# Mixture-of-experts stage: expert pairs in four 32-column strips with raw fp32 weights, in place of single experts with split weights

## The chip, the cores and the metric

The kernel runs on one core of one Trainium2 chip. The metric is device time in microseconds of one execution. Before the change three runs took 1139.29, 1140.35 and 1140.89 us (median 1140.35).

## What is computed

Two transformer blocks run one after the other on 256 tokens of width 1024. The change touches the last part of the second block alone, a hierarchical mixture of experts:

```python
def hier_moe(h, lp):
    g_logits = h @ lp['w_router_group'] + lp['b_router_group']       # 4 groups
    g_sel = argmax(g_logits); p_sel = softmax(g_logits)[g_sel]
    e_sel = (h @ lp['w_router_expert'] + lp['b_router_expert'])[group g_sel]   # 4 experts
    top_v, top_i = lax.top_k(e_sel, 2)
    w_top = softmax(top_v) * p_sel
    for e in range(16):
        a = silu(h @ w_gate[e]) * (h @ w_up[e])      # 1024 -> 512
        y = y + combine[..., e, None] * (a @ w_down[e])   # 512 -> 1024
```

Each token goes to one group of four experts and to two experts in it. Each expert has three fp32 matrices of 2 MB, so the stage reads 16 x 3 x 2 = 96 MB of weights.

## The kernel before

Up to the router the kernel runs the first block's two layers and the second block's mixer; this part has the same instructions in both kernels. The stage in question is the function `moe`.

**Precision.** A matrix product is made of three passes in the type fp32r: weights `raw` are loaded by a DMA of 1 MB, ScalarE casts them to `whi` (L191), VectorE forms the rest `wlo` (L192), and `mm3` (L247) multiplies hi by hi, hi by lo and lo by hi. The activations are split in the same way (`xgh`/`xgl`, `ahh`/`ahl`).

**Order of the work.** `route` (L1210 on) forms the logits `lt`, gives each token its group and a slot of 128 in that group (`slot`), and the weight of each expert (`comb`). `gather` (L1281) brings the tokens of two groups into slots by matmuls with a 0/1 matrix `oh`, 256 columns at a time. Then for each of 16 experts come `expert_gate`, `expert_split` (L1328 transposes), `expert_up` and `expert_out`, software-pipelined by one expert, each with 128 slots as the stationary side and 512 columns as the moving side: 72 matmuls an expert. After each group `combine` (L1354) adds the result to the tokens in `y`. `finish` (L1445 to L1457) normalizes, adds the residual and stores.

**Buffers.** All weight DMAs stand in one queue, that of SyncE (SP), in program order, each of 1 MB (`128x2048` fp32). `raw()` chooses the buffer: three in the pool `wraw`, and others in the pools `wx`, `s8` and `act3`. The split weights lie in `wsp` (three buffers of `whi` and `wlo`), which lives to the end of the kernel. `cst3`, a table of the mixer, occupies one `wraw` buffer until its last use at L982.

**Too many tokens.** When a group has over 128 tokens, a further pass runs under `If(rv > 0)` (L1421): every engine loads the flag (L1420) and branches.

Of the kernel before, what the change touches and what calls it, by code (L numbers as in the profile page):

```python
# [19 lines left out]
NEG = -1e30  # L20
SPREAD = (0, 2, 4, 6, 1, 3, 5, 7)
# [121 lines left out]
class Build:  # L143
    def __init__(self, ctx, tc, ins, out, offs, dbg=None):
        self.tc, self.nc, self.ins, self.out, self.dbg = tc, tc.nc, ins, out, dbg or {}
        self.offs, self.at = offs, {}
        pool = lambda name, bufs, **k: ctx.enter_context(tc.tile_pool(name=name, bufs=bufs, **k))
        self.const = pool("const", 1, side="right")
        self.wraw = pool("wraw", 3)
        self.psum = pool("psum", 1, space=bass.MemoryType.PSUM)  # L150
        self.pool = pool
        self.pending = None
        self.wx, self.wy, self.nraw = None, None, 0
# [40 lines left out]
    def raw(self, shape):  # L194
        n, self.nraw = self.nraw, self.nraw + 1
        if self.wx:
            i = n % 10 if n < 20 else (n - 20) % 6
            if i == 8:
                return self.big("raw", shape[1:])
            if i >= 6:  # L200
                return self.act.tile(shape, F32, tag=("xgh", "xgl", None, "yo")[i - 6], name="raw", bufs=1 if i == 9 else 2)
            if i >= 4:
                return self.wx.tile(shape, F32, tag="raw", name="raw")
        else:
            i = n % 4
        if self.wy and i == 3:
            return self.wy.tile(shape, F32, tag="raw", name="raw")
        return self.wraw.tile(shape, F32, tag="raw", name="raw")
# [1002 lines left out]
    def route(self):  # L1211
# [9 lines left out]
        rank = self.ranks(v[:, 0:2], 2, "g")  # L1221
        asg = tmp.tile([P, 2, 4], FR, tag="asg", name="asg", bufs=1)
        nc.vector.tensor_scalar(asg, rank, 0.0, None, op0=OP.is_equal)
        own = asg.bitcast(F32)
        ps = self.bank()
        nc.tensor.matmul(ps[:, 0:8], self.striu, asg.rearrange("p j g -> p (j g)"), start=True, stop=False,
                         skip_group_check=True)
        nc.tensor.matmul(ps[:, 4:8], self.onesr, asg[:, 0], start=False, stop=True, skip_group_check=True)
        self.slot = keep.tile([P, 2, 4, 4], F32, tag="slot", name="slot")[:, :, :, 0]
        nc.vector.tensor_scalar(self.slot, own, -1000.0, 1000.0, op0=OP.mult, op1=OP.add)  # L1230
        self.slotted = tt(self.slot, self.slot, ps[:, 0:8].rearrange("p (j g) -> p j g", j=2), op=OP.add)
        for j in range(2):
            nc.tensor.matmul(ps[:, 8:12], self.onesr, asg[:, j], start=j == 0, stop=j == 1, skip_group_check=True)
# [7 lines left out]
        rank = self.ranks(ve, 8, "e")  # L1241
# [19 lines left out]
        self.split(comb, *(self.idc[:, :, o:o + 16].rearrange("p j (g i) -> p j g i", g=4) for o in (P, P + 16)))  # L1261
        self.over = keep.tile([P, 5], mybir.dt.int32, tag="over", name="over")
        mxc = small("mxc", 1)
        nc.vector.tensor_reduce(mxc, ps[:, 8:12], AX.X, OP.max)
        nc.vector.tensor_scalar(self.over[:, 0:4], ps[:, 8:12], 128.0, None, op0=OP.is_gt)
        nc.vector.tensor_scalar(self.over[:, 4:5], mxc, 128.0, None, op0=OP.is_gt)

    def gather(self, p, slot):
        nc = self.nc
        oh = self.act.tile([P, 2, 2, P], FR, tag="oh", name="oh", bufs=2)  # L1270
        for j in range(2):
            nc.vector.tensor_tensor(oh[:, j], self.p("iota")[:, None, :].to_broadcast([P, 2, P]),
                                    slot[:, j, 2 * p:2 * p + 2, None].to_broadcast([P, 2, P]), op=OP.is_equal)
        X = self.hilo("xg", 8, 256, bufs=2)
        yield oh, X
        for q in range(4):
            ps = self.bank()
            for k in range(2):
                f = slice((2 * q + k) * P, (2 * q + k + 1) * P)
                for i, (j, s) in enumerate(((0, 0), (1, 0), (0, 1), (1, 1))):  # L1280
                    nc.tensor.matmul(ps[:, k * 256:(k + 1) * 256], self.H2[s][:, j, f],  # L1281
                                     oh[:, j].rearrange("p n s -> p (n s)"), start=i == 0, stop=i == 3)
            t = self.act.tile([P, 2, 256], F32, tag="xgt", name="xgt", bufs=2)
            for k in range(2):
                m = 2 * q + k
                nc.scalar.activation(t[:, k, :], ps[:, k * 256:(k + 1) * 256], AF.Identity, bias=self.cols[:, 2, m:m + 1],
                                     scale=self.cols[:, 1, m:m + 1])
            self.split(t, X[0][:, 2 * q:2 * q + 2], X[1][:, 2 * q:2 * q + 2])
            yield

    def select(self, g, oh):
        nc = self.nc
        ps = self.bank()
        for j in range(2):
            nc.tensor.matmul(ps[:, j * 160:(j + 1) * 160], oh[:, j, g % 2, :], self.idc[:, j, :], start=True, stop=True)
        v = ps[:, 0:320].rearrange("p (j s) -> p j s", j=2)
        oT = self.act.tile([P, 2, P], FR, tag="oT", name="oT", bufs=2)
        nc.scalar.copy(oT, v[:, :, 0:P])
        cw = self.act.tile([P, 4], F32, tag="cw", name="cw", bufs=2)
        for i in range(4):  # L1300
            e = 4 * g + i
            nc.vector.tensor_reduce(cw[:, i:i + 1], v[:, :, P + e:P + 32:16], AX.XY, OP.add)
        return oT, cw

    def expert_in(self, name, e, X):
        w = self.ins[name][e].rearrange("q p (k c) -> p q k c", k=4)
        n = slice(e // 4 % 2 * P, (e // 4 % 2 + 1) * P)
# [7 lines left out]
    def expert_gate(self, e, X):  # L1315
        ga = self.tmp.tile([P, 512], F32, tag="ga", name="ga")
        self.nc.scalar.activation(ga, self.expert_in("w_gate_2", e, X), AF.Silu)
        return ga

    def expert_up(self, e, X, ga, cw):  # L1320
        self.nc.vector.scalar_tensor_tensor(ga, self.expert_in("w_up_2", e, X), cw[:, e % 4:e % 4 + 1], ga,
                                            op0=OP.mult, op1=OP.mult)

    def expert_split(self, ga):
        nc = self.nc
        ps = self.bank()
        for m in range(4):
            nc.tensor.transpose(ps[:, m * P:(m + 1) * P], ga[:, m * P:(m + 1) * P], self.c("ident"))  # L1328
        A = self.hilo("ah", 4, P, bufs=2)
        self.split(ps.rearrange("p (m s) -> p m s", m=4), *A)  # L1330
        return A

    def expert_out(self, e, A, acc):
        w = self.ins["w_down_2"][e].rearrange("q p (k c) -> p q k c", k=2)
        for q in range(2):
            W = self.weights(w[:, q], 2, 1024, -2 if e else -4)
            for hf in range(2):
                self.mm3(acc[hf], [((A[0][:, 2 * q + k, :], A[1][:, 2 * q + k, :]),
                                    (W[0][:, k, hf * 512:(hf + 1) * 512], W[1][:, k, hf * 512:(hf + 1) * 512]))
                                   for k in range(2)], start=e % 4 == 0 and q == 0, stop=e % 4 == 3 and q == 1)  # L1340

    def group_out(self, acc):
# [18 lines left out]
    def moe(self, x2, h2):  # L1361
        nc = self.nc
        self.H2 = h2
        self.held = []
        self.idc = self.act.tile([P, 2, 160], FR, tag="idc", name="idc")
        so = self.tmp.tile([P, 2, P], FR, tag="ga", name="so")
# [6 lines left out]
        it = self.gather(0, self.slot)  # L1373
        got = next(it)
        with self.tc.issue_after(self.slotted.ins):
            self.h2lo()
        for _ in it:
            pass
        self.held = [self.h2hi.ins]
        ga = self.expert_gate(0, got[1])  # L1380
        sel = self.select(0, got[0])
        self.expert_up(0, got[1], ga, sel[1])
        self.held = []
        done = None
        for e in range(16):
            g = e // 4
            if e < 15:
                if e == 7:
                    for _ in it:
                        pass  # L1390
                    got = nxt
                gn = self.expert_gate(e + 1, got[1])
            if e % 4 == 0:
                acc = [self.bank("acc", 4) for _ in range(2)]
            A = self.expert_split(ga)
            if done:
                with self.later(100):
                    self.combine(y, *done)
                done = None
            if e == 13:  # L1400
                g2 = [self.act.tile([P, 512], F32, tag=f"g2{q}", name="g2") for q in range(2)]
                self.row(self.cols[:, 3, :], g2)
            if e < 15:
                nsel = self.select(g + 1, got[0]) if e % 4 == 3 else sel
                self.expert_up(e + 1, got[1], gn, nsel[1])
                ga = gn
            if e == 3:
                it = self.gather(1, self.slot)
                nxt = next(it)
# [165 lines left out]
```

## Time and profile before

| | before |
|---|---|
| median of 3 runs | 1140.35 us |
| the profiled execution | 1136.58 us |
| its span, first to last instruction | 1134.7 us |
| mean granted TensorE clock | 0.975 of full |
| TensorE busy / VectorE / ScalarE | 95% / 79% / 57% |
| read from device memory | 246.01 MB |

The profiled execution is 1.88 us longer than its span, and 3.77 us shorter than the median of the runs. Times below are counted from the first instruction of the span.

### The profile page before, as it was taken

The numbers are of one execution on the slowest core, as the hardware profiler recorded it, in microseconds if no ns is written. First come the engines' busy times: TensorE is split into PE (matmuls) and PEld (weight loads), VectorE is DVE, ScalarE is ACT, GpSimd is POOL, SyncE is SP. The second block draws the span as 40 slices with busy tenths as digits, with TensorE's granted clock in tenths as the row PEclk, the third lists the DMA queues.
The fourth block names the chain that finished last, engine by engine and source line by source line (L and its number), as shares of the span: only waits on it lengthen the run. The fifth ranks groups of instructions, "written<-read, shape, count | busy, mean of one in ns | idle before, by whom it ended". The sixth has DMA issues, their size and how long they took to land.

```text
span 1134.7 us, 18470 instructions
## 1 busy us (share of the span) xinstructions
PE 1073.8 (95%) x7384; PEld 974.0 (86%) x7384; DVE 894.6 (79%) x1448; ACT 643.5 (57%) x937; POOL 130.2 (11%) x139
## 2 busy tenths in 40 slices
PE   7997999999999989899999989899899999999995
PEld 6896999999998978899999988877788888878783
DVE  6897678888777977856877778775599888998976
ACT  5635554344455364635554345743687778777763
POOL 3190010000020930310000022000000000000001
PEclk9998999999999989989999999899899999999998
DMA  8634347776754244555667750320678689989871
GB/s 283 232 112 167 131 152 275 247 254 242 268 187 149 103 158 154 213 189 210 236 237 283 294 207 24 144 75 12 265 274 339 259 323 344 350 345 371 302 299 41
DMA packets 41390, 248.34 MB, mean 219 GB/s; under 512 B 4560, under 2 KB 6992, under 8 KB 15312
## 3 DMA queue, kind: packets, MB, share of 16 engines
q1 hardware_dynamic: 41296, 247.08, 59.0%
q8 instruction: 60, 0.98, 0.3%
q14 instruction: 34, 0.28, 0.1%
HBM read 246.01 MB, written 1.05 MB: 218 GB/s over the span
## 4 chain that ended last, share of the span: by engine, by line
PE 46%; DVE 4%; ACT 2%; issue 1%; POOL 1%; POOLq 0%; DVEq 0%; ACTq 0%
PE mm L247 23%; PE acc L247 14%; DVE wlo L192 1%; ACT whi L191 1%; PE mm L1354 1%; PE mm L1281 1%; PE mm L733 1%; PE mm L1328 1%; PE acc L922 1%; PE mm L805 0%; POOL ssq L285 0%; PE mm L1063 0%; PE mm L1064 0%; DVE Mt L757 0%; PE mm L1129 0%
## 5 line engine op out<-in xcount | busy, mean ns | idle before, releaser
L191 ACT CAST whi<-raw 128x1024 fp32r<-128x1024 f32 (+2 forms) x375 | 406.0, 1124 | 262.2 <-PE mm L247 124.7
L192 DVE TENSOR_TENSOR wlo<-raw,whi 128x1024 fp32r<-128x1024 f32 (+2 forms) x375 | 484.2, 1326 | 80.5 <-ACT whi L191 79.4
L247 PE MATMUL mm<-hfh,whi 128*128 128x256 f32 x672 | 91.5, 278 | 0.1
L247 PE MATMUL mm<-hfl,whi 128*128 128x256 f32 x672 | 90.4, 277 | 0.0
L247 PE MATMUL mm<-hfh,wlo 128*128 128x256 f32 x672 | 90.1, 277 | 0.0
L285 POOL TENSOR_TENSOR ssq<-ssq,sqt 128x256 f32<-128x256 f32 x40 | 38.2, 957 | 430.1 <-ACT sqt L277 428.8
L247 PEld LDWEIGHTS mm<-hfh,whi 128*128 128x128 f32 x672 | 83.2, 188 | 0.4 <-ACT whi L191 0.4
L247 PEld LDWEIGHTS mm<-hfl,whi 128*128 128x128 f32 x672 | 82.7, 188 | 0.0
L247 PEld LDWEIGHTS mm<-hfh,wlo 128*128 128x128 f32 x672 | 82.7, 188 | 0.0
L247 PE MATMUL acc<-ffh,whi 128*128 128x256 f32 x352 | 72.0, 285 | 0.0
L247 PE MATMUL mm<-whi,xgh 128*128 128x512 f32 x256 | 71.7, 399 | 0.4 <-ACT xgh L191 0.3
L247 PE MATMUL acc<-ffh,wlo 128*128 128x256 f32 x352 | 71.0, 283 | 0.0
L247 PE MATMUL acc<-ffl,whi 128*128 128x256 f32 x352 | 70.7, 282 | 0.0
L247 PE MATMUL mm<-wlo,xgh 128*128 128x512 f32 x256 | 70.4, 395 | 0.0
L247 PE MATMUL mm<-whi,xgl 128*128 128x512 f32 x256 | 70.0, 395 | 0.0
L696 DVE CUSTOM_DVE_ANT_0 araw<-araw,arow 128x1024 f32<-128x1024 f32 x48 | 58.5, 1231 | 0.0
L247 PEld LDWEIGHTS mm<-wlo,xgh 128*128 128x128 f32 x256 | 47.9, 187 | 11.9 <-DVE wlo L192 0.3
L247 PEld LDWEIGHTS mm<-whi,xgl 128*128 128x128 f32 x256 | 48.0, 187 | 11.7
L247 PEld LDWEIGHTS mm<-whi,xgh 128*128 128x128 f32 x256 | 46.8, 188 | 11.7 <-ACT xgh L191 1.2
L247 PEld LDWEIGHTS acc<-ffh,whi 128*128 128x128 f32 x352 | 55.0, 192 | 0.2
L247 PEld LDWEIGHTS acc<-ffl,whi 128*128 128x128 f32 x352 | 54.8, 191 | 0.0
L247 PEld LDWEIGHTS acc<-ffh,wlo 128*128 128x128 f32 x352 | 54.8, 191 | 0.0
(489 smaller groups left out, 2034.8 us busy)
## 6 DMA issues: line engine op xcount, KB each, us to landing
raw<-in_w_gate_dram SPq DMA_DIRECT2D x54, 1024.0 KB, 5.4
raw<-in_w_up_dram SPq DMA_DIRECT2D x54, 1024.0 KB, 5.2
raw<-in_w_down_dram SPq DMA_DIRECT2D x54, 1024.0 KB, 4.9
raw<-in_w_in_dram SPq DMA_DIRECT2D x29, 1024.0 KB, 4.9
araw<-in_w_adaT_dram SPq DMA_DIRECT2D x48, 512.0 KB, 5.0
raw<-in_w_out_dram SPq DMA_DIRECT2D x12, 1024.0 KB, 4.8
x<-in_xT_dram SPq DMA_DIRECT2D x4, 256.0 KB, 5.5
raw<-in_w_in_dram SPq DMA_DIRECT2D x4, 256.0 KB, 5.6
```

The lines of the kernel that those rows point to most:

```text
L191: nc.scalar.copy(hi, src)
L192: nc.vector.tensor_tensor(lo, src, hi.bitcast(F32), op=OP.subtract)
L247: self.nc.tensor.matmul(out, w, x, start=start and i == 0, stop=stop and i == n - 1, **kw)
L285: nc.gpsimd.tensor_tensor(self.ssq, self.ssq, sq, op=OP.add)
L696: nc.vector.tensor_tensor_reduce(out, raw, rows[n], 1.0, 0.0, OP.mult, OP.add, self.mod[:, t, n:n + 1])
L733: nc.tensor.matmul(ps[0:100, :], self.weff[:, (c + 4) % 8, :], src, start=c == 0, stop=c == 7)
L922: nc.tensor.matmul(psx[m][:, 0:258], a, b[:, k, :], start=k == 0 and i == 0, stop=k == 7 and i == 2)
L1281: nc.tensor.matmul(ps[:, k * 256:(k + 1) * 256], self.H2[s][:, j, f], oh[:, j].rearrange("p n s -> p (n s)"), start=i == 0, stop=i == 3)
L1328: nc.tensor.transpose(ps[:, m * P:(m + 1) * P], ga[:, m * P:(m + 1) * P], self.c("ident"))
L1354: nc.tensor.matmul(ps, oT[:, j, :], Y[:, s, hf, :], start=s == 0, stop=s == 1)
```

## The change

Expert p (of groups 0 and 1) and expert 8+p (of groups 2 and 3) form pair p, of eight. The 128 slots of a pair are four strips of 32: strips 2 and 3 belong to the first expert, strip 1 to the second, and strip 0 to the second if it has over 32 tokens, else to the first. `quads` multiplies each strip, 32 stationary columns, with the weights of its expert, and its output goes to 32 partitions of PSUM. Weights and gathered tokens stay fp32 and are not split. The host lays the weights out so that one 1 MB tile holds both experts of a pair. Raw weights go through a ring of 3 + 13 buffers; the pool `wsp` is closed before the stage. `gather` runs for two pairs at once, four times in all instead of twice. `route` counts tokens by expert. Tokens over a pair's room are done in up to three later rounds, each under an `If` of its own.

```diff
+RING = (6, 7, 11, 8, 1, 4, 2, 5, 0, 3, 9, 10, 12)
...
+        if self.ring:
+            i = n % (3 + len(self.ring))
+            if i >= 3:
+                return self.act.tile(shape, F32, tag=f"ring{self.ring[i - 3]}", name="raw")
...
-        rank = self.ranks(v[:, 0:2], 2, "g")
+        rank = self.ranks(v, 10, "r")
+        own = small("own", 2, 4)
+        nc.vector.tensor_scalar(own, rank[:, 0:2], 0.0, None, op0=OP.is_equal)
...
+        nc.vector.tensor_scalar(self.side, ps[:, 40:48], 32.0, None, op0=OP.is_gt)
...
+                for i, (j, s) in enumerate(((0, 0), (1, 0), (0, 1), (1, 1))):
+                    nc.tensor.matmul(o, self.H2[s][:, j, m * P:(m + 1) * P],
+                                     oh[:, j, 0:n].rearrange("p n s -> p (n s)"), start=i == 0, stop=i == 3)
...
+    def pair(self, name, p, q):
+        w = self.raw([P, 2, 2, 512])
+        self.nc.sync.dma_start(w, self.ins[name][p, q].rearrange("p (e k c) -> p e k c", e=2, k=2))
+        return w
+
+    def sides(self, p):
+        v = self.nc.values_load(self.side[0:1, p:p + 1], engines=(mybir.EngineType.PE,), min_val=0, max_val=1)
+        return [bass.ds(v, 1), slice(1, 2), slice(0, 1), slice(0, 1)]
+
+    def quads(self, out, x, w, side, start, stop):
+        for t in range(4):
+            r = slice(32 * t, 32 * t + 32)
+            self.nc.tensor.matmul(out[r], x[:, r], w[:, side[t]].rearrange("p e c -> p (e c)"), start=start, stop=stop)
+
+    def pair_in(self, name, p, X, side):
         ps = self.bank()
-        for q in range(2):
-            W = self.weights(w[:, q], 4, 512, -2 if e else -4, self.held if q else ())
-            self.mm3(ps, [((X[0][:, 4 * q + k, n], X[1][:, 4 * q + k, n]), (W[0][:, k, :], W[1][:, k, :]))
-                          for k in range(4)], start=q == 0, stop=q == 1)
+        for q in range(4):
+            w = self.pair(name, p, q)
+            for k in range(2):
+                self.quads(ps, X[:, 2 * q + k], w[:, :, k, :], side, q == 0 and k == 0, q == 3 and k == 1)
         return ps
...
+    def pair_out(self, p, A, side):
         Y = self.act.tile([P, 2, 2, 512], FR, tag="yo", name="yo")
         for hf in range(2):
-            self.split(acc[hf], Y[:, 0, hf, :], Y[:, 1, hf, :])
+            acc = self.bank("acc", 4)
+            for q in range(2):
+                w = self.pair("w_down_2", p, 2 * hf + q)
+                for k in range(2):
+                    self.quads(acc, A[:, 2 * q + k], w[:, :, k, :], side, q == 0 and k == 0, q == 1 and k == 1)
+            self.split(acc, Y[:, 0, hf, :], Y[:, 1, hf, :])
         return Y
...
+        for r in range(3):
+            rv = nc.values_load(self.over[0:1, 3, r:r + 1])
+            with self.tc.If(rv > 0):
...
+                for p in range(8):
+                    rp = nc.values_load(self.over[0:1, r, p:p + 1])
+                    with self.tc.If(rp > 0):
...
         phb.close()
+        phw.close()
         pha.close()
```

The DMA queue of SP (each row one or more 1 MB transfers, with the semaphores that it waits for; the mixer's four `w_out` tiles stand just ahead). Before, the first expert tiles stood so:

```order
L234 DMA raw<-in_w_up_dram 128x2048 [waits DMAHW5_49,DVE_49,Activation_49]
L234 DMA raw<-in_w_gate_dram 128x2048 [waits DMAHW7_49,DVE_49]
L234 DMA raw<-in_w_gate_dram 128x2048 [waits DMAHW4_49,PE_49]
L234 DMA raw<-in_w_up_dram 128x2048 [waits DMAHW0_49,DVE_49]
L234 DMA raw<-in_w_gate_dram 128x2048 [waits DMAHW2_49,DVE_49]
L234 DMA raw<-in_w_gate_dram 128x2048 [waits Pool_49]
L234 DMA raw<-in_w_gate_dram 128x2048
L234 DMA raw<-in_w_down_dram 128x2048 [waits DVE_49]
L234 DMA raw<-in_w_down_dram 128x2048 [waits DMAHW1_49]
L234 DMA raw<-in_w_up_dram 128x2048 [waits PE_49]
```

And so they stand now:

```order
L1339 DMA raw<-in_w_gate_dram 128x2048 [waits DMAHW7_49,DVE_49]
L1339 DMA raw<-in_w_gate_dram 128x2048 [waits DMAHW4_49,PE_49]
L1339 DMA raw<-in_w_gate_dram 128x2048 [waits DMAHW0_49,DVE_49]
L1339 DMA raw<-in_w_gate_dram 128x2048 [waits DMAHW5_49,PE_49]
L1339 DMA raw<-in_w_up_dram 128x2048 [waits Pool_49]
L1339 DMA raw<-in_w_up_dram 128x2048 x2
L1339 DMA raw<-in_w_up_dram 128x2048 [waits PE_49]
L1339 DMA raw<-in_w_gate_dram 128x2048 [waits DMAHW1_49]
L1339 DMA raw<-in_w_gate_dram 128x2048 [waits DMAHW2_49]
L1339 DMA raw<-in_w_gate_dram 128x2048 [waits DMAHW3_49]
L1339 DMA raw<-in_w_gate_dram 128x2048 [waits DMAHW4_49]
```

The first up tile ahead of the gate tiles is gone. The first three gate tiles wait for what the second, third and fourth tile waited for before: the splits of two `w_out` tiles (DVE) and, between them, the last use of `cst3` at L982 (PE). The fourth waits for the last matmul with the second `w_out` tile, the next three for something long past (Pool), the eighth for the last matmul of `w_out` (PE). Eight more follow that wait for no computation but one small Pool operation of the router's normalization, and from the seventeenth on each waits for the matmuls that read the tile sixteen places ahead of it.

On TensorE, in the middle of the stage (`cst_160` with `ga` are the transposes between up and down, `yo` with `oT` the combine), the rows before were these:

```order
L247 MATMUL mm<-wlo,xgh 128x512
L247 MATMUL mm<-whi,xgl 128x512 x4
L1328 MATMUL mm<-cst_160,ga 128x128 x4
L1354 MATMUL mm<-yo,oT 128x512
L247 MATMUL mm<-whi,xgh 128x512 [waits Activation_49]
L247 MATMUL mm<-whi,xgh 128x512
L247 MATMUL mm<-whi,xgh 128x512 [waits Activation_49]
L247 MATMUL mm<-whi,xgh 128x512
L247 MATMUL mm<-wlo,xgh 128x512 [waits DVE_49]
```

And these are they now, where `ISA` sets the register that chooses the expert of strip 0, and a waiting row with the x3 row behind it is one quad:

```order
L1349 ISA
L1349 MATMUL acc<-raw,ah 32x512 x4
L1349 ISA
L1349 MATMUL mm<-raw,xg 32x512 [waits DMAHW5_49,DVE_49]
L1349 MATMUL mm<-raw,xg 32x512 x3
L1349 ISA
L1349 MATMUL mm<-raw,xg 32x512 x4
L1372 MATMUL mm<-cst_160,ga 128x128 [waits DVE_49]
L1372 MATMUL mm<-cst_160,ga 128x128 x3
L1393 MATMUL mm<-yo,oT 128x512 [waits DVE_49,Activation_49]
```

Where the engine waited for the two casts of a tile it now waits for the tile's DMA, and one tile of 1 MB feeds two quads. For each pair there are 24 quads, 96 matmuls of 32 x 512; for the same two experts there were 144 of 128 x 512.

## Rows read from the trace of the kernel before

**Rows 1.** The page, parts 1 and 2 (busy time, 40 slices of 28.4 us):

```profile
PE 1073.8 (95%) x7384; PEld 974.0 (86%) x7384; DVE 894.6 (79%) x1448; ACT 643.5 (57%) x937; POOL 130.2 (11%) x139
...
GB/s 283 232 112 167 131 152 275 247 254 242 268 187 149 103 158 154 213 189 210 236 237 283 294 207 24 144 75 12 265 274 339 259 323 344 350 345 371 302 299 41
```

**Rows 2.** Windows: length, then busy PE, PEld, DVE, ACT, POOL; clock, DMA share, GB/s.

```profile
765.00:795.00 30.00, 28.59 (x179) 23.55 (x180) 17.13 (x62) 9.37 (x24) 1.38 (x2) 1.00 0.07 22
812.00:830.00 18.00, 14.72 (x76) 13.44 (x75) 13.23 (x54) 13.84 (x31) 1.52 (x2) 0.62 0.62 240
850.00:870.00 20.00, 20.00 (x90) 16.12 (x89) 19.09 (x22) 15.68 (x20) 0.00 (x0) 1.00 0.99 381
1035.00:1050.00 15.00, 15.00 (x69) 12.17 (x68) 13.11 (x17) 11.58 (x15) 0.00 (x0) 1.00 0.99 395
1080.00:1100.00 20.00, 20.00 (x98) 16.48 (x97) 16.72 (x16) 13.72 (x16) 0.00 (x0) 1.00 0.89 342
```

**Rows 3.** Chain that ended last, in the stage: start us, us, what.

```profile
830.19 2.61 PE mm L247 x10
...
847.79 5.59 PE mm L247 x24
...
905.27 0.94 PE mm L1281 x8
...
1063.24 1.98 PE mm L1354 x8
```

**Rows 4.** Timeline of the last 20 us: start us, us, instruction.

```profile
1118.80 0.63 PE L247 MATMUL acc<-whi,ahl 128*128 128x512 f32 x2
...
1120.88 2.48 DVE L1359 TENSOR_TENSOR y<-mm,y 128x512 f32<-128x512 f32 x4
```

**Rows 5.** Groups by line and form, 823 to 1124 us: busy us, mean ns.

```profile
L192 DVE TENSOR_TENSOR wlo<-raw,whi 128x1024 fp32r<-128x1024 f32 x180 | 210.5, 1221 | 17.5 <-ACT whi L191 17.2
L191 ACT CAST whi<-raw 128x1024 fp32r<-128x1024 f32 x180 | 179.6, 1050 | 43.0 <-PE mm L247 26.5 <-PE acc L247 15.8 <-ACT whi L191 0.7
```

**Rows 6.** Waits of SP's queue, 700 to 1135 us: us, times, longest.

```profile
SPq L234 <- DVE wlo L192: 299.4, 92, 14.5
SPq L234 <- PE acc L982: 39.1, 1, 39.1
```

**Rows 7.** Timeline of TensorE, single places: start us, us, instruction, count of records.

```profile
28.94 1.02 PE L381 MATMUL mm<-ropeb,cst 128*128 128x512 f32 x2
...
85.67 0.66 PE L538 MATMUL mm<-wsT,ones 128*64 128x128 f32 x8
...
798.57 0.62 PE L247 MATMUL acc<-wlo,m2h 128*128 128x512 f32 x2
...
811.17 0.62 PE L247 MATMUL acc<-whi,m2l 128*128 128x512 f32 x2
...
1108.61 0.60 PE L1328 MATMUL mm<-cst,ga 128*128 128x128 f32 x4
```

**Rows 8.** Lines L380 (form of L381), L538, L1328: ns of a record, min/median/max.

```profile
L380 PE MATMUL mm<-ropea,cst x12: 590/592/592, 22.7 to 383.5; 128*128 128x512 f32 x12
...
L538 PE MATMUL mm<-wsT,ones x16: 272/273/323, 85.7 to 402.9; 128*64 128x128 f32 x16
...
L1328 PE MATMUL mm<-cst,ga x64: 270/272/273, 847.2 to 1108.9; 128*128 128x128 f32 x64
```

**Rows 9.** Lines L1420 and L1421 on SP, the flag's load and branch: ns, start us.

```profile
L1420 SPq TENSOR_LOAD <-over x1: 482/482/482, 1129.7 to 1129.7; - x1
...
L1421 SPq EVENT_SEMAPHORE  x9: 17/17/17, 1132.7 to 1133.3; - x9
```

**Rows 10.** Timeline of SP's queue around the stage's start: start us, us, issues.

```profile
752.46 39.80 SPq L234 DMA_DIRECT2D raw<-in_w_gate_dram  x2
798.52 0.33 SPq L234 DMA_DIRECT2D raw<-in_w_up_dram  x1
```

**Rows 11.** DMA issues: count, KB each, median us from issue to landing.

```profile
raw<-in_w_gate_dram SPq DMA_DIRECT2D x54, 1024.0 KB, 5.4
```

More of the change, by code (lines that the diff above doesn't have):

```diff
@@ new lines, in route @@
+        self.slot = keep.tile([P, 2, 8], F32, tag="slot", name="slot")
+        put = small("put", 2, 2, 8)
+        for h, b in enumerate((64.0, 32.0)):
+            nc.vector.tensor_scalar(put[:, :, h], before[:, :, h], b, -2 * b, op0=OP.is_ge, op1=OP.mult)
+            nc.vector.scalar_tensor_tensor(put[:, :, h], before[:, :, h], b, put[:, :, h], op0=OP.add, op1=OP.add)
+        full = small("full", 2, 2, 8)
+        nc.vector.tensor_scalar(full, past, 0.0, 1000.0, op0=OP.is_ge, op1=OP.mult)
@@ L1266, in route @@
-        nc.vector.tensor_scalar(self.over[:, 4:5], mxc, 128.0, None, op0=OP.is_gt)
-    def gather(self, p, slot):
-        nc = self.nc
[L1270 to L1275, printed above, removed]
+        pairs = small("pairs", 2, 2, 4)
@@ new lines, in route @@
+        tt(pairs, comb[:, :, 0:2], comb[:, :, 2:4], op=OP.add)
+        self.split(pairs, *(self.idc[:, :, o:o + 8].rearrange("p j (g i) -> p j g i", g=2) for o in (P, P + 8)))
+        self.over = keep.tile([P, 4, 8], mybir.dt.int32, tag="over", name="over")
+        most, big = small("most", 8), small("big", 1)
+        tt(room, ps[:, 32:48].rearrange("p (h e) -> p h e", h=2), room, op=OP.subtract)
+        tt(most, room[:, 0], room[:, 1], op=OP.max)
+        nc.vector.tensor_reduce(big, most, AX.X, OP.max)
@@ L1372, in moe @@
         y = self.big("y", (2, 1024))
-        it = self.gather(0, self.slot)
-        got = next(it)
+        oh = self.hot(0)
         with self.tc.issue_after(self.slotted.ins):
             self.h2lo()
[L1377 to L1383, printed above, removed]
-        done = None
[L1385 to L1395, printed above, removed]
+        X = dict(enumerate(self.gather(oh)))
+        side = {0: self.sides(0)}
+        ga = {0: self.pair_gate(0, X[0], side[0])}
+        sel = {p: self.select(p, oh) for p in range(2)}
+        self.pair_up(0, X[0], side[0], ga[0], sel[0][1])
+        done = None
+        for p in range(8):
+            if p < 7:
+                side[p + 1] = self.sides(p + 1)
+                ga[p + 1] = self.pair_gate(p + 1, X[p + 1], side[p + 1])
+            A = self.pair_turn(ga[p])
             if done:
@@ L1398, in moe @@
                     self.combine(y, *done)
-                done = None
-            if e == 13:
+            if p == 6:
                 g2 = [self.act.tile([P, 512], F32, tag=f"g2{q}", name="g2") for q in range(2)]
                 self.row(self.cols[:, 3, :], g2)
[L1403 to L1409, printed above, removed]
@@ L1410, in moe @@
-            if 3 <= e < 7:
-                next(it, None)
-            self.expert_out(e, A, acc)
-            if e % 4 == 3:
-                done = (sel[0], self.group_out(acc), g == 0)
-                sel = nsel
+            if p < 7:
+                self.pair_up(p + 1, X[p + 1], side[p + 1], ga[p + 1], sel[p + 1][1])
+            if p % 2 == 0 and p < 6:
+                oh = self.hot(p + 2)
+                X[p + 2], X[p + 3] = self.gather(oh)
+                for n in range(p + 2, p + 4):
+                    sel[n] = self.select(n, oh)
@@ new lines, in moe @@
+        side = [slice(0, 1)] * 2 + [slice(1, 2)] * 2
+        for r in range(3):
+            rv = nc.values_load(self.over[0:1, 3, r:r + 1])
+            with self.tc.If(rv > 0):
+                late = self.tmp.tile([P, 2, 2, 8], F32, tag="sl2", name="sl2", bufs=1)
+                nc.vector.tensor_scalar(late, self.late, -64.0 * r, None, op0=OP.add)
+                for p in range(8):
+                    rp = nc.values_load(self.over[0:1, r, p:p + 1])
+                    with self.tc.If(rp > 0):
+                        oh = self.hot(p, late)
+                        X = self.gather(oh, 1)[0]
+                        oT, cw = self.select(p, oh, 0)
+                        ga = self.pair_gate(p, X, side)
+                        self.pair_up(p, X, side, ga, cw)
+                        self.combine(y, oT, self.pair_out(p, self.pair_turn(ga), side))
+                self.finish(x2, y, yg, g2)
```

178 lines of the change are left out of this document (83 added, 95 removed).

## Prediction, made before the change was run

> **What bounds the kernel now.** I read the page first, then the stage in windows, its chain and its groups, and last the DMA queue. The page [rows 1] shows TensorE at 95% of the span, and transfers that stay high only from the 29th slice on, which is the changed stage. In the stage's windows [rows 2] TensorE is busy in every microsecond at granted clock 1.00, while the DMA engines' share is 0.89 to 0.99: both are nearly full. The chain says which one ends last: it runs over TensorE, 24 matmuls for one product in 5.59 us [rows 3], so 0.233 us a matmul. 16 experts x 72 matmuls x 0.233 = 268 us of the 289 us between the first expert matmuls of the chain, 830.2 [rows 3], and the last, 1119.4 [rows 4]. VectorE and ScalarE split weights meanwhile, 180 pieces of 1.22 and 1.05 us [rows 5], and SP's queue waits mostly for such a split to free a buffer, 299 us in 92 waits [rows 6]. That costs nothing as long as TensorE is full.
>
> **What the change makes of TensorE.** The 16 x 72 matmuls go, and 8 x 24 = 192 quads come. No row shows four strips of 32 columns, so the price q of a quad has to be bounded. An fp32 matmul stands in the trace as two records, one for each of its passes: L381, 512 columns, takes 1.02 us [rows 7], a record of this form 0.59 [rows 8], so the second starts 0.43 us after the first, and a matmul in a row of such costs 0.86 us. Four one after the other would be 3.45 us. Two strips do have a row: L538 (stationary side 128x64, output in two halves in turn), eight records in 0.66 us [rows 7], each 0.27 [rows 8], so one starts every (0.66 - 0.27) / 7 = 0.055 us. The transposes L1328, 128 columns too but over the whole width, start every (0.60 - 0.27) / 3 = 0.11 us [rows 7, 8]. Two strips thus ran fully side by side. The bounds for four are q = 0.86 (all at once) and q = 1.72 (two and two). I take 0.86, since two strips lost nothing against one.
>
> The rest of TensorE's work: 4 gathers of 32 matmuls at 0.94 / 8 = 0.118 us, 15.1; 64 combine matmuls at 1.98 / 8 = 0.248, 15.9 [rows 3]; 8 x 4 transposes in two records each, 8 x 2 x 0.60 = 9.6 at most [rows 7]; 32 small `select` matmuls, at most as dear as a combine, 8. Together 48.6. If the experts begin where they begin now, at 830.2 [rows 3], TensorE is done at 878.8 + 192 q, which is 1044 for q = 0.86.
>
> The register settings (`ISA`) have no row. A load from a tile takes SP 0.48 us [rows 9], so the eight of `side` about 4 us; the settings should pass while 0.86 us of matmuls run. I take nothing for either, because TensorE will wait for transfers; without that cover the loads would cost their 4 us, and the settings up to 0.05 us each (the spacing that TensorE reaches in L538), 10 us.
>
> **What the change makes of the transfers.** The bytes stay: 96 tiles of 1.0486 MB. What held them back goes, since a tile is free when its own matmuls are done, and there are 16 buffers. The first tile goes at 752.5, the next behind the one wait of 39.1 us for the last use of `cst3`, at 792.2 [rows 6, 10]. That wait stays, and it leaves the DMA engines idle: 22 GB/s from 765 to 795 [rows 2]. The third goes at 798.5 [rows 10]; the fourth waits for matmuls that end at 799.2 [rows 7], and the next three for nothing. So five tiles, 13.6 us of transfer at the pace below, are under way by 801, and the next nine may go when `w_out` is done, 811.8 [rows 7], in time. The third lands 5.4 us after its issue [rows 11], at 803.9, and from there the stream is unbroken if buffers come free in time. Its pace is that of the windows where the share is 0.99: 381 and 395 GB/s [rows 2]. I take 385, which is 2.72 us a tile. The sixteenth tile lands at 803.9 + 13 x 2.72 = 839.3, and the first two quads free a buffer at 832 to 837, so the queue has work. The 93 tiles after the third are in at 803.9 + 93 x 2.72 = 1056.9. That is later than 1044: **the transfers become the bound**, and TensorE waits for tiles.
>
> Bounds of the pace: 395 / 0.99 = 399 GB/s, 2.63 us, would give 1048; the window at a share of 0.89, 342 GB/s [rows 2], 3.07 us, gives 1089.
>
> **The route.** Ranking by expert and counting rooms now stand ahead of `slot`, and the gather and all experts are queued behind it. These small operations of VectorE have no rows in this arrangement. I take 0 to 5 us, hidden while the buffers fill until 839; each microsecond beyond that moves the end by as much.
>
> **The end.** From the last expert matmul, 1119.4 [rows 4], to the span's end are 15.3 us. Now the last tile is followed by two quads, 1.7 us; of the four additions to `y`, 2.48 us [rows 4], two come earlier, -1.2. And three flags are asked in turn where there was one. On SP one takes from its load at 1129.7 to the last semaphore at 1133.3 [rows 9], 3.6 us, of which the load is 0.48. Two more cost between 0 (if the next load follows at once) and 8 us (if other engines are somewhat slower). I take 7, the row's own price. The end is 1056.9 + 1.7 + 15.3 - 1.2 + 7 = 1079.7.
>
> **The sum.** The span falls by 55.0, from 1134.7 to 1079.7. The profiled execution was 1136.58, so it becomes 1081.6; the median of the runs lies 3.8 above the profiled one: 1085.4, rounded to **1086 us**.
>
> Nothing else moves: until the router all engines have the instructions of before but for splits, and the 210 and 180 us of splits [rows 5] that vanish lay beside TensorE.
>
> **Rivals.**
>
> *The transfers don't keep full pace.* For: in the stage's slices they made 259 to 371 GB/s [rows 1]. Against: there the queue waited for splits [rows 6], and at a share of 0.99 it made 381 and 395. At 342 GB/s the last tile lands 32 us later: 1118 us. The Trainium skill, "DMA: Bandwidth & Descriptors", section Bandwidth, puts a 1 MB transfer at 341 GB/s and a core's part of the memory at about 358; by that the stage would end as in this rival. The trace disagrees with it as a ceiling: 395 GB/s over 15 us of 1 MB tiles [rows 2].
>
> *A quad costs somewhat more, or the clock falls at times.* The forecast has the last quads end at 1058.6, so TensorE decides above q = 0.94. At 1.08 it ends at 1086, 28 later: 1113 us. For: TensorE now waits in each tile, and where it waited, 812 to 830, the granted clock was 0.62 on average [rows 2], a mixture of the levels 2.4 and 1.2 GHz; a quarter of the quads at 1.2 GHz gives q = 1.08. Against: a TensorE that falls behind stops waiting, and in the full windows the clock is 1.00. The Trainium skill, "TensorE: Matmul & The Clock Gate", Part 3, has three column strips gain 2.38, not 3. By that an estimate is q = 0.86 x 3 / 2.38 = 1.08. No run here shows three strips.
>
> *Only two of the four strips go side by side* (the other sign). Place: every quad, since each strip has a stream of its own from all 128 partitions, and no row shows more than two such streams. At q = 1.72 TensorE ends at 1209, and 21.1 later the span at 1230: 1236 us. It is slower than before once TensorE ends after 1113.6, which is q above 1.22.
>
> *The change doesn't do what it says*: a pair has more tokens than room, and a round fetches its 12 tiles again, 12 x 2.72 = 33 us, with a second `finish`: some 1130 us. The reference's router on its inputs gives at most 81 tokens to a first expert (room 96) and 40 to a second with room 64, so no round should run.
>
> **Chances.** Forecast 0.60; lower pace 0.14; dearer quads under 1.22, 0.13; two and two 0.10; extra rounds 0.03. The forecast's own range is 1070 (399 GB/s, no price of the flags) to 1102 (362 GB/s). My range reaches from there to the two rivals near 1115: 1068 to 1120. A measurement of this kernel tells 0.2% (2.3 us) from no change. Faster: 0.60 + 0.14 + 0.12 + 0.02 = 0.88; same 0.02; slower 0.10.
>
> **What would show it.** Right: windows from 850 to 1050 at 375 GB/s or more with a DMA share near 1.00 and TensorE under 90% busy; L1349's matmuls waiting for DMAs; quads 0.86 us apart where two follow without a wait; the last weight tile landing near 1057, and 23 us from there to the end. Wrong: TensorE busy throughout with quads at 1.1 us or more (the strips); a DMA share under 0.9 with SP waiting for TensorE (the ring is too short, or the start late); a granted clock well under 1.00. The price of a quad is the likeliest to make it wrong, since it rests on a row with two strips.

## The result, and the profile after

The changed kernel took 1075.59 us in the median of four runs (1073.18 to 1080.94); the kernel before took 1139.82 in the median of its four. The ratio is 0.945, 95% interval 0.941 to 0.950. The forecast was 1086 us, the range 1068 to 1120. The profiled execution took 1075.02 us, its span is 1073.2.

The page, as in [rows 1]: busy time of TensorE, VectorE and ScalarE, then the transfers in slices of 26.8 us.

```profile
PE 995.1 (93%) x7840; PEld 818.4 (76%) x7840; DVE 676.7 (63%) x1266; ACT 449.3 (42%) x721; POOL 129.8 (12%) x139
...
GB/s 283 261 113 123 145 156 244 262 250 245 273 237 184 79 163 113 195 230 163 221 250 211 288 256 246 79 138 40 41 95 412 374 420 420 420 422 420 421 320 47
```

The split work has left VectorE and ScalarE. Transfers are at 420 GB/s from the 33rd slice to the 38th, more than any slice before. Windows, as in [rows 2]:

```profile
765.00:795.00 30.00, 28.54 (x179) 23.26 (x178) 16.67 (x62) 9.10 (x23) 2.07 (x3) 1.00 0.03 5
812.00:830.00 18.00, 10.81 (x54) 9.73 (x53) 12.43 (x68) 7.55 (x20) 1.52 (x2) 0.60 0.99 402
850.00:870.00 20.00, 19.21 (x167) 7.92 (x159) 2.87 (x5) 2.64 (x6) 0.00 (x0) 1.00 1.01 422
890.00:910.00 20.00, 20.00 (x176) 6.74 (x172) 4.71 (x7) 1.76 (x3) 0.00 (x0) 1.00 1.02 421
1010.00:1030.00 20.00, 19.06 (x160) 7.71 (x156) 3.86 (x6) 2.83 (x5) 0.00 (x0) 1.00 1.01 419
1030.00:1050.00 20.00, 17.88 (x136) 4.94 (x128) 5.94 (x9) 2.59 (x6) 0.00 (x0) 1.00 0.51 212
```

Both engines look full, TensorE (second column) and the transfers (last two). Which one is the bound is told by who waits for whom. These are TensorE's waits from 834 to 1060 us, all that the trace has: total, times, longest.

```profile
PE mm L1313 <- ACT xg L1320: 3.1, 6, 0.7
PE mm L1393 <- ACT yo L192: 2.8, 4, 0.7
PE mm L1372 <- DVE ga L1365: 0.9, 1, 0.9
```

No transfer stands in it: **TensorE never waits for a tile**. (The rows of its weight loads, PEld, put nine idle stretches, 3.0 us in all, down to a transfer, but to up tiles ahead of `acc` and down tiles ahead of `mm`, which these matmuls don't read.) The trace has the landing of each transfer, and tiles are used in the order in which they are fetched. The seventeenth lands at 842.5 and is used at 871.3; the 81st lands at 1005.3, used at 1008.9; the last lands at 1042.5 (issued at 1022.8, 19.8 us earlier) and is used at 1048.5. So the lead melts from 29 to 6 us, and to 3.2 at the 88th tile, where it is smallest, but is not used up. The transfers are done in the last window above, where they fall to 212 GB/s, and TensorE is not. Accordingly the chain that ended last, as in [rows 3], runs over TensorE through the whole stage (start us, us, what):

```profile
829.65 4.48 PE mm L1313 x24
834.13 0.98 PE mm L1349 x2
...
843.38 13.87 PE mm L1349 x128
...
871.40 7.00 PE acc L1349 x64
878.40 1.72 PE mm L1349 x16
880.71 0.93 PE mm L1393 x4
881.63 1.85 PE mm L1349 x16
```

A quad is eight records (four matmuls in two passes), so 128 records in 13.87 us are 16 quads at 0.867, and 16 records in 1.72 are two at 0.86. After a few combine matmuls two take 1.85. SP's waits, as in [rows 6]:

```profile
SPq L1339 <- PE mm L1349: 55.8, 31, 17.2
SPq L1339 <- PE acc L977: 39.1, 1, 39.1
SPq L1339 <- DMA raw<-in_w_gate_dram: 35.1, 17, 2.1
SPq L1339 <- DMA raw<-in_w_down_dram: 32.5, 16, 3.6
SPq L1339 <- DMA raw<-in_w_up_dram: 31.1, 18, 2.1
```

Issue to landing, columns as in [rows 11], but of the stage's tiles alone, those issued from 845 to 1050 us (in the kernel before the same window has 5.3 to 5.6 us):

```profile
raw<-in_w_down_dram SPq DMA_DIRECT2D x28, 1024.0 KB, 19.8
raw<-in_w_gate_dram SPq DMA_DIRECT2D x24, 1024.0 KB, 18.5
raw<-in_w_up_dram SPq DMA_DIRECT2D x24, 1024.0 KB, 19.6
```

The splits of expert weights hold SP no more (two waits for the splits of `w_out` tiles, 28.7 us, remain ahead of the stage). It waits for the matmuls of L1349 and for earlier transfers, so several are under way; the wait for the last use of `cst3` (L977 now) is 39.1 us as before.

At the end the three flags are seen on SP. L1446 is the flags' line (L1420 and L1421 in [rows 9]); its branches run from 1061.4 to 1068.9:

```profile
L1446 SPq EVENT_SEMAPHORE  x27: 17/17/17, 1064.0 to 1071.9; - x27
L1446 SPq COMPARE_BRANCH  x3: 45/45/50, 1061.4 to 1068.9; - x3
```

### The profile page after: what moved, and what is told of

Same layout as the page of the kernel before. It is cut to its first block, busy times and chain, and to the rows that moved or that the text cites. A ratio compares the mean times of both kernels' runs of the same rounds, so it can differ in the third digit from the quotient of the medians.

```text
span 1073.2 us, 19115 instructions
## 1 busy us (share of the span) xinstructions
PE 995.1 (93%) x7840; PEld 818.4 (76%) x7840; DVE 676.7 (63%) x1266; ACT 449.3 (42%) x721; POOL 129.8 (12%) x139
## 4 chain that ended last, share of the span: by engine, by line
PE 42%; DVE 5%; ACT 3%; issue 1%; POOL 1%; POOLq 0%; DVEq 0%; ACTq 0%
PE mm L1349 11%; PE mm L242 9%; PE acc L242 7%; PE acc L1349 5%; PE mm L1313 2%; PE mm L1393 2%; DVE wlo L193 1%; PE mm L728 1%; PE acc L917 1%; PE mm L1372 0%; POOL ssq L280 0%; PE mm L800 0%; PE mm L1058 0%; PE mm L1059 0%; ACT whi L192 0%
## 5 line engine op out<-in xcount | busy, mean ns | idle before, releaser
L192 ACT CAST whi<-raw 128x2048 fp32r<-128x2048 f32 (+1 forms) x171 | 213.2, 1272 | 221.3 <-PE mm L242 98.6
L193 DVE TENSOR_TENSOR wlo<-raw,whi 128x2048 fp32r<-128x2048 f32 (+1 forms) x171 | 257.2, 1518 | 63.7 <-ACT whi L192 62.8
L1349 PE MATMUL mm<-raw,xg 128*32 128x512 f32 (+1 forms) x1024 | 116.6, 594 | 0.1
L1349 PEld LDWEIGHTS mm<-raw,xg 128*32 128x32 f32 x1024 | 31.2, 110 | 69.3 <-issue 66.7
L1365 DVE SCALAR_TENSOR_TENSOR ga<-mm,cw,ga 128x512 f32<-128x512 f32 x8 | 6.0, 751 | 83.6 <-PE mm L1349 64.2
L1349 PE MATMUL acc<-raw,ah 128*32 128x512 f32 (+1 forms) x512 | 57.6, 594 | 0.0
L1349 PEld LDWEIGHTS acc<-raw,ah 128*32 128x32 f32 x512 | 15.6, 110 | 35.0 <-issue 33.2
L426 POOL TENSOR_TENSOR cv<-cv,ctap 128x256 f32<-128x256 f32 x34 | 38.1, 1122 | 21.4 <-DVE cv L428 18.9
## 6 DMA issues: line engine op xcount, KB each, us to landing
raw<-in_w_up_dram SPq DMA_DIRECT2D x54, 1024.0 KB, 12.7
```

What stands on the lines that cost most here:

```text
L192: nc.scalar.copy(hi, src)
L193: nc.vector.tensor_tensor(lo, src, hi.bitcast(F32), op=OP.subtract)
L426: nc.gpsimd.tensor_tensor(cv[:, m, :], cv[:, m, :], tp, op=OP.add)
L1349: self.nc.tensor.matmul(out[r], x[:, r], w[:, side[t]].rearrange("p e c -> p (e c)"), start=start, stop=stop)
L1365: self.nc.vector.scalar_tensor_tensor(ga, self.pair_in("w_up_2", p, X, side), cw, ga, op0=OP.mult, op1=OP.mult)
```

## The experiments

Theory A, from the profile after: TensorE is the bound. From its first quad at 834 us its own queue sets the end, and the transfers are some us ahead (6 us at the last tile by the landings, where the expectations below say 7). Theory B, the forecast's: transfers are the bound. Each of the kernels below is the changed kernel with one edit. A time with a ratio is the median of four or six runs, and the ratio, with its 95% interval, is to the kernel before on the same chip; a time without one is a single run. Differences between kernels that ran on different chips go by these ratios.

**Four kernels on one chip.** The changed kernel again:

> The changed kernel again, as the yardstick for the three kernels below that run on the same chip. Expected: 1075.6 us, within 4 us (its runs so far went from 1073.2 to 1080.9).

It took 1074.38 us (ratio 0.9445, 0.942 to 0.947).

**Fewer transfers.**

```diff
-            w = self.pair(name, p, q)
+            w = self.pair(name, p, q) if q < 3 else w
...
-                w = self.pair("w_down_2", p, 2 * hf + q)
+                w = self.pair("w_down_2", p, 2 * hf + q) if hf + q < 2 else w
```

> Leaves out 24 of the 96 weight transfers of the stage: in each product the last tile is not fetched and TensorE multiplies with the tile before it again, so all matmuls stay. Theory A (TensorE's own queue, which starts at 834 us and has no wait for a tile in it, is the bound): nothing, within 3 us of the changed kernel. Theory B (the forecast's: the transfers are the bound and TensorE waits for tiles): at 2.5 us a tile 24 of them are 60 us, of which TensorE, then the bound, lets at least 15 through.

1073.40 us (0.9433, 0.941 to 0.946): 1.0 less than the changed kernel beside it, although a quarter of the stage's bytes is gone and the transfers are down to 2 GB/s in the window from 1010 to 1030 us. Theory B falls. (The edit also moves TensorE's matmuls in its queue: 13 combine matmuls come behind the last quads, where the repeat has 4, and the waits for ScalarE and VectorE fall from 6.9 to 1.2 us. So the 1.0 is not a clean price of the transfers.)

**Less of TensorE.**

```diff
-                for i, (j, s) in enumerate(((0, 0), (1, 0), (0, 1), (1, 1))):
+                for i, (j, s) in enumerate(((0, 0), (1, 0))):
...
-                for s in range(2):
-                    nc.tensor.matmul(ps, oT[:, j, :], Y[:, s, hf, :], start=s == 0, stop=s == 1)
+                nc.tensor.matmul(ps, oT[:, j, :], Y[:, 0, hf, :], start=True, stop=True)
```

> Leaves out TensorE work and nothing else: the passes with the rest (lo) halves in the gather and in the combine, 4 x 16 matmuls at 0.136 us and 32 at 0.28 us, together 17.7 us. Theory A: TensorE ends earlier, but only until the last tile, which lands 7 us ahead of its matmuls, has to be waited for: 6 to 8 us less than the changed kernel. Theory B: only what lies behind the last tile goes, 1 to 2 us.

1068.34 us (0.9404, 0.937 to 0.944), 6.0 less. From the first quad to the last store's issue the trace has 218.7 us, where the changed kernel beside it has 224.8. And now TensorE does wait for tiles, 2.9 us in five places:

```profile
PE acc L1349 <- DMA raw<-in_w_down_dram: 1.6, 3, 0.6
...
PE mm L1349 <- DMA raw<-in_w_gate_dram: 0.8, 1, 0.8
```

The last tile lands 0.5 us ahead of its use, where it was 6.8. The two limits have met.

**Both at once.**

> Leaves out both, the 24 transfers and the 17.7 us of TensorE work. Theory A: with the transfers out of the way all of the work shows, 15 to 18 us less than the changed kernel. Theory B: the gain of the 24 transfers alone, with nothing from the smaller TensorE work.

1057.95 us (0.9294, 0.927 to 0.932), 16.4 less, where the two edits alone took 1.0 and 6.0. The cleanest comparison is with the kernel of fewer transfers, whose edit differs from this one by the TensorE work alone: 15.4 us less. With the transfers out of the way nearly all of the 17.7 us shows. (From the first quad to the last store's issue the profiled execution has 211.6 us against 224.8; the first of the four gathers lies ahead of that.) Theory A holds on all three: TensorE is the bound, with the transfers a few us behind it.

**What the strips are worth.**

```diff
-        for t in range(4):
-            r = slice(32 * t, 32 * t + 32)
-            self.nc.tensor.matmul(out[r], x[:, r], w[:, side[t]].rearrange("p e c -> p (e c)"), start=start, stop=stop)
+        for t in range(2):
+            self.nc.tensor.matmul(out, x, w[:, t], start=start and t == 0, stop=stop and t == 1)
```

> Each quad of four 32-column strips becomes two matmuls with all 128 slots as the stationary side, one for the weights of either expert (their results are summed without regard to which expert a slot belongs to, so the mixture's values are not the reference's). Transfers, buffers and the order of the work stay. If the strips are what the change gains by: two matmuls of 0.86 us in the place of one such time, 192 x 0.86 = 165 us, so about 1240 us, above the kernel before. If raw weights and the ring were what counts: near 1075 us.

1229.56 us in one run, 154 over the changed kernel. The chain gives the price:

```profile
849.04 27.51 PE mm L1348 x64
```

32 matmuls of 0.86 us, so a pair of them costs 1.72. The prediction's upper bound of a quad is thus the price of full-width matmuls, and its "two and two" rival comes out at 1230 us, where it had 1236. Raw weights and the ring without the strips lose 8% against the kernel before.

**The strips' order.**

```diff
+        for t in range(4):
+            r = slice(32 * t, 32 * t + 32)
+            for k in range(2):
+                self.nc.tensor.matmul(out[r], X[:, m + k, r], w[:, side[t], k, :].rearrange("p e c -> p (e c)"),
+                                      start=start and k == 0, stop=stop and k == 1)
```

> Same matmuls, other order: each strip multiplies its two row blocks of a tile one after the other, before the next strip comes, so that neighbours in the queue often share a strip. If TensorE starts matmuls in the order of the queue and a strip takes one at a time, two neighbours of different strips still meet, but not four: five times 0.86 us a tile less what the next tile's first strip overlaps, 3.44 us in the place of 1.72, so 96 x 1.72 = 165 us more, about 1240 us. If each strip has a queue of its own: near 1075 us.

1080.05 us in one run, and the queue theory falls: from the first quad to the last, the trace has 217.7 us against 216.4. Of the 5.0 us by which its span is longer, 3.7 lie ahead of the first quad (837.8, not 834.1; the logits are done at 824.0, not 821.2) and 1.3 behind it. The matmuls of strip 0 are the only ones whose moving address comes from a register, which their records show. By the edit four records of strip 0 (two row blocks, two passes) now stand in a row in the queue; in the trace they start at 896.403, 896.833, 897.262 and 897.691, one in every group of four records that start 30 ns apart. So matmuls of other strips start ahead of strip 0's, behind which they stand: as far as the starts tell, each strip works off its own matmuls beside the others.

**A shorter ring.**

```diff
-            i = n % (3 + len(self.ring))
+            i = n % (3 + min(SHORT, len(self.ring)))
```

With `SHORT = 5`:

> The ring has 3 + 5 buffers in the place of 3 + 13; nothing else changes. What the sixteen bought, by the theory that TensorE is the bound with 7 us in hand: the lead that transfers win while TensorE is not yet there. With eight, tile 9 can go only when the first quads free a buffer, near 836 us; 88 tiles at 2.50 us from there land at 1056, 15 us later than now, of which 7 are in hand: 8 to 12 us more than the changed kernel. If the sixteen bought nothing: within 2 us of it.

1089.57 us (0.9579, 0.956 to 0.960): 14 over the changed kernel, 15 by the ratios, more than the 8 to 12 expected. The lead is gone, 153 GB/s from 812 to 830 us in place of 402, and TensorE waits for tiles 19 times, 11.2 us in all. The pace stays: windows between 850 and 1050 us have 419 to 424 GB/s. This kernel is the place where theory B's bound would be.

**Why the pace was 420 and not 385.** First suspicion, the splits:

```diff
         w = self.raw([P, 2, 2, 512])
+        for i in range(1 + q % 2):
+            self.nc.scalar.copy(self.idle[:, 0], self.idle0)
+            self.nc.vector.tensor_tensor(self.idle[:, 1], self.idle0, self.idle0, op=OP.subtract)
```

> Adds work that nobody reads: for two tiles each three copies on ScalarE and three subtractions on VectorE of 128 x 1024, from and to buffers of their own, about three quarters of the load that the splits made in the kernel before (the ring loses one of its sixteen buffers to the scratch). Theory: the splits' traffic in the on-chip memory is why transfers made 381 and 395 GB/s before and 420 now. Then the windows from 850 us on fall to about 390 GB/s, the last tile lands 15 us later, and the time is 7 to 12 us over the changed kernel. Rival: the pace comes from a deeper queue alone; then 420 GB/s stays and the time is within 3 us of the changed kernel.

1125.80 us (0.9889, 0.987 to 0.991), far over what either side gave; but the pace did not fall. Windows, columns as above:

```profile
850.00:870.00 20.00, 20.00 (x188) 6.13 (x192) 19.41 (x21) 19.49 (x23) 0.00 (x0) 1.00 1.01 423
890.00:910.00 20.00, 19.92 (x172) 6.45 (x170) 19.59 (x19) 19.55 (x22) 0.00 (x0) 1.00 1.02 422
930.00:950.00 20.00, 14.01 (x104) 7.37 (x97) 17.73 (x18) 18.18 (x22) 0.00 (x0) 0.83 0.84 336
```

With VectorE and ScalarE busy 19.4 us of 20 the transfers make 423 and 422 GB/s, so load of this kind on the two engines is not the cause. The added work reads a small buffer over and over, though; that reading the tiles themselves slows the transfers was not tried. The 50 us have another cause: the small operations that TensorE needs stand behind the added ones in the two engines' queues. TensorE's waits come to 43.0 us from 830 to 1110, where the changed kernel has 6.8.

```profile
PE mm L1396 <- ACT yo L192: 11.8, 6, 6.5
PE mm L1313 <- DVE ga L1368: 9.3, 2, 5.4
PE mm L1313 <- DVE pairs L1281: 6.7, 1, 6.7
```

Where TensorE waits so, its granted clock falls too, to 0.83 on average in the third window, between its levels of 2.4 and 1.2 GHz.

Second suspicion, the number of transfers under way, with `SHORT = 1` in the ring's edit:

> The ring has 3 + 1 buffers in the place of 3 + 13. It asks why transfers made 420 GB/s where 385 was forecast. If the number of transfers under way sets the pace: with four buffers, of which TensorE holds one or two, two or three are under way, a transfer takes 5 to 6 us from issue to landing as in the kernel before, and the windows from 850 us on show 340 to 395 GB/s at a share near 1.0, so 1110 to 1180 us. If the pace has another cause, it stays at 420 GB/s where TensorE doesn't hold it back, and the time is near that of the ring of eight, 1090 us.

1109.79 us in one run, just under the range for few transfers. Issue to landing is 7.8 to 7.9 us for the tiles issued from 845 to 1050, not 5 to 6, and the pace changes from window to window:

```profile
890.00:910.00 20.00, 15.66 (x134) 3.46 (x135) 1.31 (x2) 1.73 (x3) 0.00 (x0) 1.00 1.01 421
1010.00:1030.00 20.00, 17.00 (x138) 5.34 (x140) 2.58 (x4) 1.19 (x2) 0.00 (x0) 1.00 0.99 388
1050.00:1070.00 20.00, 16.86 (x145) 5.51 (x145) 2.13 (x3) 2.94 (x5) 0.00 (x0) 1.00 0.99 386
```

Half of the expectation is met: with few buffers windows of 381 to 388 GB/s come back, at a share of 0.96 to 0.99, as in the kernel before; but others keep 417 to 423, more than was expected of four buffers. With the ring of eight no window fell so, though TensorE was idle there too:

```profile
1010.00:1030.00 20.00, 15.99 (x136) 4.24 (x132) 2.64 (x4) 1.76 (x3) 0.00 (x0) 1.00 1.01 421
```

In the full-width kernel, where SP issues one tile as one comes free, a share of 0.87 moves only 301 GB/s:

```profile
850.00:870.00 20.00, 20.00 (x48) 8.79 (x47) 0.76 (x2) 0.00 (x0) 0.00 (x0) 1.00 0.87 301
```

**The flags.**

```diff
-        for r in range(3):
-            rv = nc.values_load(self.over[0:1, 3, r:r + 1])
-            with self.tc.If(rv > 0):
+    def rounds(self, r, x2, y, yg, g2, side):
+        nc = self.nc
+        rv = nc.values_load(self.over[0:1, 3, r:r + 1])
+        with self.tc.If(rv > 0):
...
+            if r < 2:
+                self.rounds(r + 1, x2, y, yg, g2, side)
```

> The later rounds stand one inside the other, since a round's flag can only be set when the one before it is: then only the first flag is asked when no round runs. Nothing is left out. By the forecast's price of a flag, 3.5 us, two fewer are worth 7 us: 1068.5 us. If the loads of the flags and the branches lay beside the last stores: nothing.

1066.86 us (0.9381, 0.936 to 0.941). By the ratio to the kernel before (0.9445 above) 7.3 us less, with intervals that don't overlap but leave some 3 to 11 us. In the trace the last store is issued 5.4 us ahead of the end, where it was 14.2 (13.4 in the repeat).

**An earlier start, and all together.**

```diff
         self.route()
+        g2 = [self.act.tile([P, 512], F32, tag=f"g2{q}", name="g2") for q in range(2)]
+        self.row(self.cols[:, 3, :], g2)
...
+        with self.later(60):
+            self.weigh(v, rank, own, ps, room, small)
```

`weigh` is the part of `route` behind `late`, unchanged.

> Nothing is left out, two things move. The row of the last normalization (g2, some 1.8 us of TensorE's work) goes from the seventh pair to the route, where TensorE waits; and the small operations on VectorE for the weights and the flags go behind the second half of the slot matrix and the rest of the tokens, which the gather waits for (1.4 us). Theory A (TensorE is the bound from its start on, with 7 us in hand against the transfers): 2 to 4 us less than the changed kernel. Theory B (the transfers): nothing.

1073.17 us (0.9419, 0.939 to 0.944). By the ratio 3 us less, with intervals that overlap. The profiled executions agree: from the end of the logits to the first quad 11.1 us in place of 12.9, and from there to the last quad's end 215.1 in place of 216.4.

> The edits of the two kernels before together, as a candidate for the fastest version. Theory A: both gains, 9 to 11 us less than the changed kernel, about 1065 us. If one gain uses up the slack of the other: 7 us.

1062.76 us (0.9347, 0.932 to 0.937), the fastest version here: about 11 us below the changed kernel by the ratios, 6.5% below the kernel before. That the two gains add up is not shown: the interval overlaps that of the kernel with one flag, and in the profiled execution the earlier start is gone. From the end of the logits to the first quad are 12.7 us again, because the moved row (L1171) now stands in the chain ahead of the gather (start us, us, what):

```profile
820.79 3.63 PE mm L1171 x16
824.93 5.01 PE mm L1319 x24
```

What stays is 1.4 us between the first quad and the last quad's end (215.0). The transfers are close behind: the last tile lands 3.2 us ahead of its use, the 88th only 0.4.

## Why the prediction came out right, and where it did not

**The price of a quad** was right: 0.86 us taken, 0.86 to 0.87 measured, up to 0.93 behind other matmuls. The row with two strips [rows 7] did carry over to four. The Trainium skill, "TensorE: Matmul & The Clock Gate", Part 3, has 2.38 for three strips; the trace disagrees for four of this kind, which lose nothing: 13.87 us for 16 quads, where one strip's matmuls alone would take 16 x 0.86 by the price of L381 [rows 7, 8].

**The rest of TensorE** was 48.6 us in the forecast. From the first quad to the last quad's end are 216.4 us, of which 192 x 0.86 = 165.1 are quads, so 51 for the rest. The forecast's 48.6 also held the first gather, which lies ahead of the first quad (a fourth of 15.1), and four combine matmuls behind the last (1.0); like with like, 44 were taken. Some 6 us of the stretch are the waits for small operations shown above, for which the forecast took nothing.

**The settings and loads of registers** were put at nothing because TensorE would be waiting for transfers. It wasn't, so the reason was wrong and the term right by luck: the settings lie beside the matmuls of the quad before, and of the eight loads, 0.29 to 0.49 us each, four lie at 826.6 to 829.3, while TensorE waits for the route, and four at 862.9 to 865.6, with 0.11 us of idle time in the chain.

**Its start** was mis-sized: 830.2 was kept, 834.1 came. The logits end at 821.2, 1.3 later than before; from their end to the gather are 8.4 us where the trace of before has 3.4 (819.93 to 823.37), 5.0 more and the upper end of the 0 to 5 that the forecast gave to the route; and the first matmuls follow the gather 2.3 us sooner, since nothing is split: 4.0 in sum. The forecast hid the route behind the filling buffers until 839. With TensorE as the bound it was not hidden.

**"The transfers become the bound"** is the step that failed. The third tile landed at 804.6 (forecast 803.9), so the start of the stream was right. The pace was not: 2.50 us a tile, 420 GB/s, against 2.72, and beyond the lower bound of 2.63 too. Nor was the stream unbroken. The sixteenth tile landed at 839.0, as forecast (839.3), but by luck: the eighth was issued only at 813.1, behind `w_out`, and such pauses took what the faster pace gave. Then all sixteen buffers were full, SP waited 17.2 us for the first quads, and from 830 to 850 us the transfers made 358 GB/s. So the mean from the third tile to the last is 2.56 us. The last tile landed at 1042.5, not 1056.9. TensorE, which the forecast had done at 1044, was done at 1050.4 and became the bound. The two lie so close that the error cost little: the last quads ended 8 us earlier than forecast (1050.4, not 1058.6). That the time came out within 1% with the wrong resource as the bound is luck. Two of the forecast's own signs of being right did not come: TensorE is 95 to 100% busy in the windows from 850 to 1030 us, not under 90%, and L1349's matmuls wait for no DMA.

The pace was misread in a definite way. 381 and 395 GB/s stood beside a DMA share of 0.99 [rows 2], and the forecast took that as full. The runs show that it wasn't: the same engines make 420 at a share of 1.01 and 386 at 0.99, with the ring of four. Issue to landing tells the kernels apart. 5.4 us [rows 11] at 385 GB/s are 2.1 MB, two tiles under way; in the changed kernel 18.5 to 19.8 us at 420 are about 8 MB, eight tiles; with the ring of four 7.9 us at 386 to 421 are three, and the pace comes and goes. With the ring of eight (16.1 to 17.6 us, some seven tiles) it is full throughout. So few transfers under way are the cause as far as the rings of four, eight and sixteen show, and the number from which the pace stays full lies above three and at seven or less. The load that copies and subtractions put on ScalarE and VectorE is excluded; that splits read the tiles themselves was not tried apart. The Trainium skill, "DMA: Bandwidth & Descriptors", section Bandwidth, has 425 GB/s for 16 MB in one transfer beside the 341 for 1 MB that the prediction quoted. The trace agrees with the larger one: 420 GB/s with about eight 1 MB transfers under way.

**The flags** were right: 7 us taken, 7.3 measured by taking two away (some 3 to 11 by the intervals), and some 3.75 from one branch to the next on SP. **The end**: from the last quad to the span's end 22.8 us, 21.1 forecast.

**The sum.** Span 1073.2 against 1079.7, so 6.5 of the 10 us between forecast and median are the 8 us at the last quads less the 1.7 at the end. Most of the other 4 are the 3.8 us by which the median of the runs before lay above its profiled execution; here the median lies 0.6 above.

**The rivals.** None came. A lower pace: the pace was higher. Dearer quads: no, and TensorE stopped waiting, as the argument against that rival said; the granted clock is 1.00, the level of 2.4 GHz, in the windows from 850 to 1050 us. Two and two: no, but its price and time are what full-width matmuls have. Extra rounds: none ran, 54 tiles of each kind are fetched as before.

## What to carry to other kernels

When two resources are forecast to end within some 15 us of each other, work out both ends and say which error turns them round: here a pace 9% higher did, with the pauses of the stream 6%. A busy share of the DMA engines near 1.0 does not mean that they are at their pace; look at the time from issue to landing times the rate, which is the amount under way, and take the pace from a stretch in which several transfers are under way. And an `If` that is never taken still costs its flag, some 3.7 us each here: ask one that covers the others.

## What was not expected of the hardware

Four fp32 matmuls of 32 stationary columns ran wholly beside each other: their records start 7 ns apart (896.154, 896.161, 896.167, 896.174), and the next four 0.43 us later. The order in which the strips' matmuls stand in the queue made hardly a difference to it (16 quads in 13.94 us in place of 13.87). One core held 419 to 422 GB/s of reads for 180 us. And the settings of the register that chooses strip 0's expert, 192 of them at 51 to 65 ns, cost nothing that shows: they lie beside the matmuls of the quad before.
